# One order of steps for the opening of a hybrid transformer block: products of ones, half of u's first block between v's tiles, two low parts on GpSimd

## The chip, the cores and the metric

The kernel runs on one NeuronCore of a Trainium2 chip. Five engines work side by side, each through its own queue in program order: TensorE (PE, with its weight loads PEld), VectorE (DVE), ScalarE (ACT), GpSimd (POOL) and SyncE (SP, which here issues most DMAs). They meet only through semaphores. The metric is the device time of one execution in microseconds (us), lower is better. The kernel before takes 1760.06 us, the median of three runs (1760.02 to 1760.11).

## The reference

The reference is one layer of a hybrid decoder on x of 1024 rows by 1024 channels, in float32:

```python
h = rms_norm(x, attn_norm_w)
q, k, v, u, g = split(h @ w_in)          # 1024, 1024, 1024, 2048, 2048 columns
a = diff_attention(rms(q), rms(k), v)    # 8 heads, causal, with a position bias
y_a = (rms_norm(a) * (1 - lam_init)) @ w_proj_attn
u_a, u_b = split(u)
c = silu(layer_norm(causal_conv31(u_a * sigmoid(u_b)) + conv_b))
y_b = c @ w_proj_conv
g_a, g_b = split(sigmoid(g + gate_b))
x = x + (g_a * y_a + g_b * y_b) @ w_out
x = x + swiglu(rms_norm(x, ffn_norm_w))  # w_gate_up, w_down
```

The change lies in the first two lines: the row norm, and the first of the products with w_in.

## The kernel before, in words

**Precision.** Every large product is made of three: each operand is split into a high part (a cast to fp32r on ACT, `split_hi`, L119) and a low part (the rest, a subtraction on DVE, `split_lo`, L124), and PE adds high by high, high by low and low by high into one PSUM bank (L152 to L154).

**The opening.** x comes in eight tiles of 128 rows. For each, `xtile` (L622) runs `norm_T` (L606): a square with a row sum on ACT (L609), the row statistic on DVE with a root on ACT (L603, L573 to L578), a multiplication by it and by the norm weights on DVE in two halves (L613), eight transposes on PE (L616), and the split into `hT_hi` and `hT_lo`, the normed rows with channels on the partitions. The norm weights arrive as one load that repeats them on all partitions (`anw_b`, 512 KB, L173, ACT's queue).

**The items.** The first phase walks a list of items: "V0" is 256 columns of v for all eight row tiles (24 products of 256 columns each, `v_item`, L633), "U0" is channels 0 to 127 of u_a and u_b for two blocks of 512 rows (four times 24 products of 512 columns, `u_item`, L539), "Q0" a head of q and k. The list begins V0, U0, U1, V1. V0 prepares the row tiles as it goes. An item stops (yields) after each group of products, and after each stop 3.25 taps of the 31-tap convolution go to DVE. Weights come through `Stream` (L293): a load of 512 KB into one of two raw buffers (`wraw`), then the split; `ahead` says how many are prepared before they are used.

**What sets the order.** The program is recorded, and a scheduler then puts the instructions of each engine in an order, so work of later items can stand between that of earlier ones; `after(ins)` (L126) holds what is recorded inside it behind a given instruction. In the opening before, nothing is held: V's tiles, the preparation of later tiles, U0's products, the small vectors (L200 to L230) and the position bias rows (`bias_rows`, L661) are woven together by the scheduler.

After the first phase come attention with the remaining items (318 to about 825 us), the projections, and the channel mixer.

## Time and profile before

| | us |
|---|---|
| median of three runs | 1760.06 |
| the profiled execution, as a run | 1761.41 |
| its span, first to last instruction | 1759.6 |
| PE busy in the span | 1740.3 |
| DVE busy | 1273.2 |
| ACT busy | 800.5 |
| POOL busy | 26.7 |

Busy time is the sum of an engine's instructions without their overlap. PE's products overlap, so one product's price is read from the distance between two starts. A row of the timeline gives start, duration, engine, source line, operation, output and inputs, shapes, and in square brackets how long the engine had been idle before it and what released it. "xN" merges N like instructions. In lists of waits the columns are total, times, and the longest. A table of windows gives each engine's busy time (and count) per stretch of the span.

### The profile page before, as it was taken

What the parts mean: (1) busy time and instruction counts of PE and PEld (TensorE: products, weight loads), DVE (VectorE), ACT (ScalarE), POOL (GpSimd) and SP (SyncE); (2) the same over time, 40 slices, a digit from 0 to 9 for tenths busy, and PEclk for the clock granted to TensorE, in tenths of its full rate; (3) what the DMA queues carried; (4) which work ended last, traced back from release to release, by engine and by line L of the source; (5) the groups of instructions that cost most, each with busy time, mean ns of one, the idle gap of its engine ahead of it and who ended that gap; (6) DMA issues with size and microseconds to landing.
All of it is one profiled execution on the core that took longest, in us unless ns stands there. A gap on an engine that the chain in (4) does not pass through costs nothing.

```text
span 1759.6 us, 25844 instructions
## 1 busy us (share of the span) xinstructions
PE 1740.3 (99%) x9367; PEld 1503.1 (85%) x9367; DVE 1273.2 (72%) x2187; ACT 800.5 (45%) x1886; POOL 26.7 (2%) x106
## 2 busy tenths in 40 slices
PE   7999999999999999999999999999999999999999
PEld 6898998988999998988888888888888888888887
DVE  6388879999988888886687534877667666664544
ACT  4211241558767776655557313643333333333332
POOL 3000000000000000000000000000000000000000
PEclk9999999999999999999999999999999999999999
DMA  8433353235444344352983544234544544697663
GB/s 248 164 121 114 108 158 124 76 96 151 111 138 124 88 114 138 86 163 76 336 268 108 168 167 144 91 102 146 177 150 158 176 157 139 210 360 242 215 216 131
DMA packets 255728, 275.34 MB, mean 156 GB/s; under 512 B 16064, under 2 KB 177896, under 8 KB 255600
## 3 DMA queue, kind: packets, MB, share of 16 engines
q1 hardware_dynamic: 253568, 267.45, 47.6%
q0 software_dynamic: 1744, 5.19, 1.0%
q8 instruction: 74, 1.21, 0.3%
q10 hardware_dynamic: 288, 1.05, 0.2%
q14 instruction: 54, 0.44, 0.1%
HBM read 176.59 MB, written 78.68 MB: 145 GB/s over the span
## 4 chain that ended last, share of the span: by engine, by line
PE 95%; DMA 2%; ACT 1%; DVE 1%; issue 0%; SPq 0%; ACTq 0%
PE acc L1375 22%; PE pg L153 15%; PE pg L154 15%; PE pg L152 15%; PE acc L451 12%; PE sc L817 2%; PE sc L816 2%; PE wo L154 2%; PE wo L153 2%; PE wo L152 2%; PE pT L852 2%; PE pW L152 1%; PE pW L154 1%; PE pW L153 1%; PE pQ L714 1%; DMA wraw<-in_w_in_dram 1%
## 5 line engine op out<-in xcount | busy, mean ns | idle before, releaser
L525 DVE SCALAR_TENSOR_TENSOR acc<-u,cw,acc 128x1024 f32<-128x1024 f32 x240 | 306.8, 1278 | 2.8
L152 PE MATMUL pg<-whi,hT_hi 128*128 128x256 f32 x768 | 220.3, 287 | 1.2 <-ACT hT_hi L119 1.2
L154 PE MATMUL pg<-whi,hT_lo 128*128 128x256 f32 x768 | 219.8, 286 | 0.4 <-DVE hT_lo L124 0.4
L153 PE MATMUL pg<-wlo,hT_hi 128*128 128x256 f32 x768 | 219.1, 285 | 0.2 <-DVE wlo L124 0.2
L119 ACT CAST whi<-wraw 128x1024 fp32r<-128x1024 f32 x109 | 114.4, 1051 | 215.9 <-PE pg L153 122.1
L152 PE MATMUL pg<-hT_hi,whi 128*128 128x512 f32 x512 | 201.6, 394 | 0.0
L154 PE MATMUL pg<-hT_hi,wlo 128*128 128x512 f32 x512 | 200.9, 393 | 0.0
L153 PE MATMUL pg<-hT_lo,whi 128*128 128x512 f32 x512 | 200.5, 392 | 0.0
L124 DVE TENSOR_TENSOR wlo<-wraw,whi 128x1024 fp32r<-128x1024 f32 x109 | 132.8, 1219 | 70.8 <-ACT whi L119 66.7
L124 DVE TENSOR_TENSOR wlo<-draw,whi 128x1024 fp32r<-128x1024 f32 x75 | 91.8, 1224 | 89.6 <-ACT whi L119 84.3
L152 PEld LDWEIGHTS pg<-whi,hT_hi 128*128 128x128 f32 x768 | 147.7, 192 | 4.2 <-ACT hT_hi L119 2.5
L154 PEld LDWEIGHTS pg<-whi,hT_lo 128*128 128x128 f32 x768 | 147.8, 192 | 2.3 <-DVE hT_lo L124 1.1
L153 PEld LDWEIGHTS pg<-wlo,hT_hi 128*128 128x128 f32 x768 | 147.7, 192 | 2.0 <-DVE wlo L124 0.5
L119 ACT CAST whi<-draw 128x1024 fp32r<-128x1024 f32 x75 | 79.1, 1055 | 129.5 <-PE acc L451 125.9
L451 PE MATMUL acc<-wlo,whi 128*128 128x512 f32 x308 | 119.8, 389 | 0.0
L451 PE MATMUL acc<-whi,wlo 128*128 128x512 f32 x308 | 119.8, 389 | 0.0
L823 ACT ACTIVATE E<-E,mn 128x256 f32<-128x256 f32 (+7 forms) x128 | 99.7, 779 | 35.8 <-DVE mn L818 33.6
L154 PEld LDWEIGHTS pg<-hT_hi,wlo 128*128 128x128 f32 x512 | 96.2, 188 | 19.0
L153 PEld LDWEIGHTS pg<-hT_lo,whi 128*128 128x128 f32 x512 | 96.2, 188 | 18.7
L152 PEld LDWEIGHTS pg<-hT_hi,whi 128*128 128x128 f32 x512 | 96.3, 188 | 18.3
L1375 PE MATMUL acc<-h_hi,whi 128*128 128x512 f32 x240 | 93.4, 389 | 0.0
L1375 PE MATMUL acc<-h_lo,whi 128*128 128x512 f32 x240 | 93.4, 389 | 0.0
(270 smaller groups left out, 3951.5 us busy)
## 6 DMA issues: line engine op xcount, KB each, us to landing
wraw<-in_w_gate_up_dram SPq DMA_DIRECT2D x44, 512.0 KB, 4.8
wraw<-in_w_in_dram SPq DMA_DIRECT2D x40, 512.0 KB, 4.5
qs<-qs SPq DMA_DIRECT2D x96, 128.0 KB, 2.3
wd<-in_w_down_dram SPq DMA_DIRECT2D x44, 256.0 KB, 3.1
tdT<-wd SPq DMA_DIRECT2D x88, 128.0 KB, 4.3
draw<-sdS SPq DMA_DIRECT2D x44, 256.0 KB, 3.8
draw<-tdT SPq DMA_DIRECT2D x44, 256.0 KB, 3.9
wraw<-in_w_in_dram SPq DMA_DIRECT2D x32, 256.0 KB, 3.3
```

The source lines that it names most:

```text
L119: act.copy(dst, src)
L124: last_lo[0] = dve.tensor_tensor(dst, src, f32(hi), op=ALU.subtract).ins
L152: pe.matmul(o, lh, rh, start=start, stop=False)
L153: pe.matmul(o, lh, rl, start=False, stop=False)
L154: last_mm[0] = pe.matmul(o, ll, rh, start=False, stop=stop).ins
L451: m = pe.matmul(o[s_][i][:], l_[:, ts], r_[:, 512:], start=start and j + y_ == 0, stop=j == n - 1 and y_ == 2, skip_group_check=not start,)
L525: dve.scalar_tensor_tensor(acc[0][:], us[c][:, t : t + S], cw[:, c, t : t + 1], acc[0][:], op0=ALU.mult, op1=ALU.add)
L816: pe.matmul(o[:, :w], qh[:, qs], k, start=True, stop=False)
L817: last_mm[0] = pe.matmul(o[:, :w], ql[:, qs], k, start=False, stop=True).ins
L823: act.activation(e[:, :nk], e[:, :nk], AF.Exp, bias=mn[:, j : j + 1], scale=-1.0, accum_out=l[:, j : j + 1])
L852: pe.transpose(pt[:, k * P : (k + 1) * P], e[:, (k0 + k) * P : (k0 + k + 1) * P], ident[:])
L1375: pe.matmul(o[:], a_[x_][:, k, :], b_[y_][:, k, :], start=start and k + x_ + y_ == 0, stop=k == 3 and x_ == 1, skip_group_check=not start,)
```

## The change

It replaces the scheduler's order of V0 and U0 by one that is written out, `opening()`, and takes both from the list. Each of its steps is recorded inside `in_order()`, which holds it behind the last instruction of DVE, ACT and PE recorded so far. Within this:

- the norm weights arrive as two rows of 512 numbers (4 KB together), and PE spreads them over the partitions by a product with a column of ones (`spread_weights`), from where ACT copies them;
- PE multiplies a tile of ones with itself 3, 6 and 8 times (`keep_busy`), into PSUM tiles that nobody reads;
- x's first tile comes in two halves, and its square is shared by ACT and DVE; tiles 2 and 3 share one row statistic, and so do tiles 4 to 7;
- V0's weights get their own tiles, and their two low parts are made by POOL; V's 24 products of a tile are ordered high by high, low by high, high by low over all eight channel groups;
- U0 stands between V's tiles: rows 0 to 511 after V tile 3, rows 512 to 1023 after V tile 7;
- the small vectors' loads move behind POOL's low parts (`load_vectors`), their use behind V's tiles (`vectors`), and the bias rows behind what DVE and POOL had at the 16th stop. The opening stops seven times; V0 and U0 stopped eight times.

The places that the prediction speaks of, as the built programs have them. PE's first rows, before (px are the transposed rows of x's tile 0, pg V's sums):

```order
L616 MATMUL px_7_353<-ident_78,xt0_90 128x128 x4
L616 MATMUL px_8_361<-ident_78,xt0_90 128x128 x4
L152 MATMUL pg_21_398<-whi_10_370,hT_hi_334 128x256
L153 MATMUL pg_21_398<-wlo_11_371,hT_hi_334 128x256
L154 MATMUL pg_21_398<-whi_10_370,hT_lo_335 128x256
L152 MATMUL pg_21_398<-whi_10_370,hT_hi_334 128x256
```

and after, from the second row on; ahead of it stand three products of ones (pm are sums that spread the weights, or of ones):

```order
L200 MATMUL pm_14_347<-anw0_90,one_92 128x512
L200 MATMUL pm_15_350<-anw1_91,one_92 128x512
L196 MATMUL pm_16_355<-busy_93 128x512 x6
L677 MATMUL px_17_366<-ident_78,xt0_98 128x128 x4
L677 MATMUL px_18_372<-ident_78,xt0_98 128x128 x4
L833 MATMUL pg_19_380<-vwh_3_323,hT_hi_308 128x256 x4
L833 MATMUL pg_19_380<-vwh_5_325,hT_hi_308 128x256 x4
L833 MATMUL pg_19_380<-vwh_3_323,hT_lo_309 128x256 x4
L833 MATMUL pg_19_380<-vwh_5_325,hT_lo_309 128x256 x4
L833 MATMUL pg_19_380<-vwl_4_324,hT_hi_308 128x256 x4
L833 MATMUL pg_19_380<-vwl_6_326,hT_hi_308 128x256 x4
L196 MATMUL pm_20_405<-busy_93 128x512 x8
```

The transposes and V's products stand behind nine products of ones; eight more stand between tile 0 and tile 1, and the low parts of the weights (vwl) are used last.

ACT, from the casts of x's tile 3 (px_36, px_37) to u's first sigmoid, after:

```order
L120 CAST hT_hi_308<-px_36_500 128x4x128
L120 CAST hT_hi_308<-px_37_506 128x4x128
L120 CAST whi_39_537<-wraw_38_535 128x1024
L120 CAST whi_42_543<-wraw_41_541 128x1024
L120 CAST vh_45_574<-pg_19_380 128x512
L120 CAST whi_48_582<-wraw_47_580 128x1024
L652 ACTIVATE xj_51_611,ssx_50_610<-xt4_527 128x1024
L652 ACTIVATE xj_52_613,ssx_50_610<-xt5_529 128x1024
L652 ACTIVATE xj_53_615,ssx_50_610<-xt6_531 128x1024
L652 ACTIVATE xj_54_617,ssx_50_610<-xt7_533 128x1024
L609 ACTIVATE t_57_622<-v_55_619 128x4
L120 CAST vh_58_631<-pg_44_547 128x512
```

Before, from the cast of x's tile 4's first half on:

```order
L119 CAST hT_hi_334<-px_50_618 128x4x128
L609 ACTIVATE xj7_770,ss_67_771<-xt7_571 128x1024
L119 CAST vh_43_597<-pg_30_486 128x512
L119 CAST hT_hi_334<-px_51_626 128x4x128
L573 ACTIVATE t_70_776<-v_68_773 128x1
L119 CAST hT_hi_334<-px_56_671 128x4x128
L119 CAST hT_hi_334<-px_57_679 128x4x128
L545 ACT_TABLE_LOAD
L545 ACTIVATE sg_82_866<-pg_81_841 128x512
L119 CAST hT_hi_334<-px_65_731 128x4x128
```

After, the casts of three U weights (whi_39, whi_42, whi_48) stand ahead of the squares of tiles 4 to 7, and one statistic (t_57) serves all four; before, each tile's square and root stood by itself among the casts, and the U weights' casts stood elsewhere. SP's rows at the same place, after; wraw_47 is the load that whi_48 is cast from, and it takes the raw buffer of wraw_38:

```order
L287 DMA wraw_38_535<-in_w_in_dram 128x8x128
L177 DMA xt4_527<-in_x_dram 128x1024
L287 DMA wraw_41_541<-in_w_in_dram 128x8x128
L177 DMA xt5_529<-in_x_dram 128x1024
L177 DMA xt6_531<-in_x_dram 128x1024
L177 DMA xt7_533<-in_x_dram 128x1024
L287 DMA wraw_47_580<-in_w_in_dram 128x8x128
L694 DMA v_hi0_110<-vh_45_574 128x2x256
```

DVE, from the end of the row statistic of tiles 4 to 7 to the norm of tile 7, after:

```order
L614 TENSOR_TENSOR r_56_621<-r_56_621,t_57_622 128x4
L667 SCALAR_TENSOR_TENSOR xt4_527<-xt4_527,r_56_621,anw_b_101 128x512 x2
L125 TENSOR_TENSOR vl_59_632<-pg_44_547,vh_58_631 128x512
L667 SCALAR_TENSOR_TENSOR xt5_529<-xt5_529,r_56_621,anw_b_101 128x512 x2
L125 TENSOR_TENSOR hT_lo_309<-px_62_666,hT_hi_308 128x4x128
L125 TENSOR_TENSOR hT_lo_309<-px_63_672,hT_hi_308 128x4x128
L579 TENSOR_TENSOR sg_61_662<-pg_66_692,sg_61_662 128x512
L125 TENSOR_TENSOR hT_lo_309<-px_64_680,hT_hi_308 128x4x128
L125 TENSOR_TENSOR hT_lo_309<-px_65_686,hT_hi_308 128x4x128
L667 SCALAR_TENSOR_TENSOR xt6_531<-xt6_531,r_56_621,anw_b_101 128x512 x2
L667 SCALAR_TENSOR_TENSOR xt7_533<-xt7_533,r_56_621,anw_b_101 128x512 x2
```

Before, from the norm of tile 7 to u's first product with the sigmoid:

```order
L613 SCALAR_TENSOR_TENSOR xt7_571<-xt7_571,r_69_775,anw_b_92 128x512 x2
L124 TENSOR_TENSOR hT_lo_335<-px_56_671,hT_hi_334 128x4x128
L124 TENSOR_TENSOR hT_lo_335<-px_57_679,hT_hi_334 128x4x128
L124 TENSOR_TENSOR hT_lo_335<-px_65_731,hT_hi_334 128x4x128
L124 TENSOR_TENSOR vl_59_711<-pg_45_603,vh_58_710 128x512
L124 TENSOR_TENSOR hT_lo_335<-px_66_739,hT_hi_334 128x4x128
L124 TENSOR_TENSOR hT_lo_335<-px_71_784,hT_hi_334 128x4x128
L124 TENSOR_TENSOR hT_lo_335<-px_72_792,hT_hi_334 128x4x128
L124 TENSOR_TENSOR wlo_20_389<-wraw_18_386,whi_19_388 128x1024
L124 TENSOR_TENSOR vl_74_824<-pg_60_716,vh_73_823 128x512
L124 TENSOR_TENSOR wlo_77_832<-wraw_75_829,whi_76_831 128x1024
L548 TENSOR_TENSOR sg_82_866<-pg_83_868,sg_82_866 128x512
```

After, u's product with the sigmoid (sg_61, of u's sum pg_66) stands ahead of tile 5's low parts and of the norms of tiles 6 and 7; before, all norms and low parts stood ahead of it. On PE, after, the transposes of tiles 4 and 5 stand between u's first two groups of 24 products, and those of tiles 6 and 7 behind the second.

The diff, cut to its core:

```diff
+    @contextmanager
+    def in_order():
+        E = mybir.EngineType
+        with after(last_of(E.DVE)), after(last_of(E.Activation)), after(last_of(E.PE)):
+            yield
...
-    xload(0)
+    anw = [ap.tile([P, 512], F32R, tag="vh", name=f"anw{g}")[0:1, :].bitcast(F32) for g in range(2)]
+    one = ap.tile([1, P], F32, name="one", bufs=1)
+    busy = ap.tile([P, 512], F32R, tag="vl", name="busy")
+    dve.memset(f32(busy[:]), 1.0)
+    dve.memset(one[:], 1.0)
+    for g in range(2):
+        nc.scalar.dma_start(anw[g], attn_norm_w[:, 512 * g : 512 * (g + 1)])
+    xts[0] = ap.tile([P, D], F32, tag="xt", name="xt0", bufs=4)
+    for g in range(2):
+        nc.sync.dma_start(xts[0][:, 512 * g : 512 * (g + 1)], xs[0:P, 512 * g : 512 * (g + 1)])
     wb = ap.tile([P, D], F32, name="anw_b", bufs=1)
-    nc.scalar.dma_start(wb[:], attn_norm_w.to_broadcast([P, D]))
+    def keep_busy(n):
+        pt = pm()
+        for _ in range(n):
+            pe.matmul(pt[:], busy[:, :P], busy[:], start=True, stop=True)
+    def spread_weights(g):
+        pt = pm()
+        pe.matmul(pt[:], one[:], anw[g], start=True, stop=True)
+        act.copy(wb[:, 512 * g : 512 * (g + 1)], pt[:])
...
+    def load_vectors():
+        pool.memset(rows[:], 0.0)
+        pool.dma_start(cwrow[:], conv_w[0])
+        vec_rows("conv_b", conv_b, 8)
...
-    first = ["V0", "U0", "U1", "V1", "U2", "U3", "V2", "U4", "Q0", "V3", "U5", "U6", "U7"]
+    first = ["U1", "V1", "U2", "U3", "V2", "U4", "Q0", "V3", "U5", "U6", "U7"]
...
+    def u_half(c, w, sb):
+        cs = slice(sb * 512, (sb + 1) * 512)
+        ob = gemm_T(w[0], hT_hi, hT_lo, sb)
+        sg = wp.tile([P, 512], F32, tag="sg", name=nm("sg"), bufs=2)
+        act.activation(sg[:], ob[:], AF.Sigmoid)
+        yield
+        oa = gemm_T(w[1], hT_hi, hT_lo, sb)
+        dve.tensor_tensor(sg[:], oa[:], sg[:], op=ALU.mult)
+        nc.sync.dma_start(u_d[c][:, cs], sg[:])
+        if sb == 1:
+            bg.todo.insert(max(0, len(bg.todo) - CW), conv_load(c))
+            bg.add(conv_taps(c))
+        yield
     def u_item(c):
-        wb_, wa_ = ws.next(), ws.next()
+        w = ws.next(), ws.next()
         for sb in range(2):
...
+            yield from u_half(c, w, sb)
...
+    rx = {}
+    def stats(tiles):
+        n = len(tiles)
+        ss = sm.tile([P, 4], F32, tag="ssx", name=nm("ssx"), bufs=2)[:, :n]
+        for j, i in enumerate(tiles):
+            junk = ap.tile([P, D], F32, tag="junk", name=nm("xj"), bufs=1)
+            src = xts[i]
+            if i:
+                act.activation(junk[:], src[:], AF.Square, accum_out=ss[:, j : j + 1])
+            else:
+                s2 = sm.tile([P, 1], F32, tag="ss", name=nm("ss"), bufs=1)
+                act.activation(junk[:, :512], src[:, :512], AF.Square, accum_out=ss[:, j : j + 1])
+                dve.tensor_tensor_reduce(
+                    junk[:, 512:], src[:, 512:], src[:, 512:], 1.0, 0.0, ALU.mult, ALU.add, accum_out=s2[:]
+                )
+                dve.tensor_tensor(ss, ss, s2[:], op=ALU.add)
+        r = rstd_of(ss, n, 1.0 / D)
+        for j, i in enumerate(tiles):
+            rx[i] = r[:, j : j + 1]
+    def norm(i):
         for g in range(2):
-            half, gs = hbuf(g), slice(512 * g, 512 * (g + 1))
-            dve.scalar_tensor_tensor(half, src[:, gs], r, wb[:, gs], op0=ALU.mult, op1=ALU.mult)
-            pt = tp()
+            half, gs = xts[i][:, 512 * g : 512 * (g + 1)], slice(512 * g, 512 * (g + 1))
+            dve.scalar_tensor_tensor(half, half, rx[i], wb[:, gs], op0=ALU.mult, op1=ALU.mult)
+    def turn_x(i):
+        for g in range(2):
+            pt = pxp.tile([P, 512], F32, tag="px", name=nm("px"))
             for k in range(4):
-                pe.transpose(pt[:, k * P : (k + 1) * P], half[:, k * P : (k + 1) * P], ident[:])
+                c0 = 512 * g + k * P
+                pe.transpose(pt[:, k * P : (k + 1) * P], xts[i][:, c0 : c0 + P], ident[:])
             src4 = pt[:].rearrange("p (k s) -> p k s", s=P)
-            h_ = hi[:, 4 * g : 4 * g + 4, i * P : (i + 1) * P]
+            h_ = hT_hi[:, 4 * g : 4 * g + 4, i * P : (i + 1) * P]
             split_hi(h_, src4)
-            split_lo(lo[:, 4 * g : 4 * g + 4, i * P : (i + 1) * P], src4, h_)
+            turned[i, g] = src4, h_
+    def low_x(i):
+        for g in range(2):
+            src4, h_ = turned.pop((i, g))
+            split_lo(hT_lo[:, 4 * g : 4 * g + 4, i * P : (i + 1) * P], src4, h_)
...
+    def opening():
+        nonlocal qkp
+        raws = [wraw(), wraw()]
+        for g, raw in enumerate(raws):
+            nc.sync.dma_start(
+                raw[:].rearrange("p (k c) -> p k c", c=256),
+                win[512 * g : 512 * (g + 1), V0 : V0 + 256].rearrange("(k p) c -> p k c", p=P),
+            )
+        for i in range(1, 4):
+            xload(i)
+        wv = [[vw.tile([P, 1024], F32R, tag=t_, name=nm(t_)) for t_ in ("vwh", "vwl")] for g in range(2)]
+        halves = [[t_[:].rearrange("p (k c) -> p k c", c=256) for t_ in w] for w in wv]
+        uw, o = [], {}
+        def wv_hi(g):
+            split_hi(wv[g][0][:], raws[g][:])
+            pool.tensor_tensor(wv[g][1][:], raws[g][:], f32(wv[g][0][:]), op=ALU.subtract)
+        def v_tile(i):
+            if i % 2 == 0:
+                o[i // 2] = pg()
+            ts, dst = slice(i * P, (i + 1) * P), o[i // 2][:, 256 * (i % 2) : 256 * (i % 2 + 1)]
+            terms = [(k, a_, b_) for a_, b_ in ((0, 0), (1, 0), (0, 1)) for k in range(NKT)]
+            for n_, (k, a_, b_) in enumerate(terms):
+                l_, r_ = (hT_hi, hT_lo)[a_][:, k, ts], halves[k // 4][b_][:, k % 4, :]
+                last_mm[0] = pe.matmul(dst, l_, r_, start=n_ == 0, stop=n_ == len(terms) - 1).ins
+        def steps(*fns):
+            for fn in fns:
+                with in_order():
+                    fn()
+        def weight():
+            uw.append(ws.next())
+        steps(
+            lambda: keep_busy(3),
+            lambda: stats([0]),
+            lambda: spread_weights(0),
+            lambda: spread_weights(1),
+            lambda: norm(0),
+            lambda: keep_busy(6),
+            lambda: wv_hi(0),
+            lambda: wv_hi(1),
+            lambda: turn_x(0),
+            lambda: low_x(0),
+            lambda: v_tile(0),
+            lambda: keep_busy(8),
+            lambda: stats([1]),
+            lambda: norm(1),
+            lambda: stats([2, 3]),
+            lambda: turn_x(1),
+            lambda: low_x(1),
+            lambda: v_tile(1),
+            lambda: norm(2),
+            lambda: turn_x(2),
+            lambda: norm(3),
+            lambda: low_x(2),
+            lambda: turn_x(3),
+        )
+        with after(last_of(mybir.EngineType.Pool)):
+            load_vectors()
+        for i in range(4, NT):
+            xload(i)
+        steps(
+            weight,
+            lambda: v_tile(2),
+            lambda: low_x(3),
+            lambda: v_split(o[0], 0, 0),
+            weight,
+        )
+        yield
+        steps(
+            lambda: v_tile(3),
+            lambda: stats([4, 5, 6, 7]),
+            lambda: norm(4),
+            lambda: v_split(o[1], 0, 1),
+        )
+        yield
+        first_half, second_half = u_half(0, uw, 0), u_half(0, uw, 1)
+        steps(lambda: next(first_half), lambda: norm(5), lambda: turn_x(4), lambda: low_x(4), lambda: turn_x(5))
+        yield
+        steps(
+            lambda: next(first_half),
+            lambda: low_x(5),
+            lambda: norm(6),
+            lambda: turn_x(6),
+            lambda: norm(7),
+            lambda: low_x(6),
+            lambda: turn_x(7),
+            lambda: low_x(7),
+            lambda: v_tile(4),
+            lambda: v_tile(5),
+        )
+        yield
+        v_split(o[2], 0, 2)
+        steps(lambda: v_tile(6), lambda: v_tile(7), vectors)
+        v_split(o[3], 0, 3)
+        yield
+        vw_ctx.close()
+        qkp = qk_ctx.enter_context(tc.tile_pool(name="qkp", bufs=2, side="right", reuse_waits="tile"))
+        ws.ahead = 2
+        yield from second_half
+    ws.ahead = 1
     n = 0
     due = 0.0
-    for _ in run(first):
+    for _ in chain(opening(), run(first)):
         n += 1
         if n == 16:
-            bias_rows()
+            with after(last_of(mybir.EngineType.DVE)), after(last_of(mybir.EngineType.Pool)):
+                bias_rows()
         if n >= 18 and n % 3 == 0 and (n - 18) // 3 < H:
             bias_skew((n - 18) // 3)
         due += TAPS_FIRST
```

139 lines of the change are left out of this document (54 added, 85 removed).

## The prediction

> **What bounds the kernel now.** I read the page's head first, then the table of windows, then PE's waits, then the opening in order of time.
>
> ```profile
> span 1759.6 us, 25844 instructions
> core 0: us, PE busy (x) PEld busy (x) DVE busy (x) ACT busy (x) POOL busy (x), PEclk, DMA share, GB/s
> 0.00:10.00 10.00, 0.55 (x3) 0.58 (x4) 2.35 (x8) 2.63 (x4) 6.08 (x17) 1.00 0.83 218
> 10.00:20.00 10.00, 8.80 (x39) 7.64 (x37) 7.57 (x23) 7.99 (x15) 3.44 (x9) 1.00 1.01 338
> 20.00:36.00 16.00, 15.35 (x113) 12.57 (x112) 14.95 (x49) 9.25 (x21) 2.24 (x5) 1.00 0.58 179
> 36.00:94.00 58.00, 58.00 (x317) 50.40 (x315) 23.75 (x32) 15.05 (x24) 2.40 (x5) 1.00 0.55 176
> 260.00:830.00 570.00, 566.48 (x3682) 513.48 (x3681) 499.80 (x1087) 356.06 (x1201) 12.12 (x68) 1.00 0.40 117
> ```
>
> From 36 us on TensorE (PE) is busy all the time: whatever makes its opening work end earlier or later moves the end of the kernel by as much. In the opening it loses time in three ways: it starts late, it starts slowly, and it waits a little.
>
> ```profile
> PE px L616 <- DVE xt L613: 9.4, 1, 9.4
> 12.37 0.58 PE L152 MATMUL pg<-whi,hT_hi 128*128 128x256 f32 x1 [0.98 <-ACT hT_hi L119]
> 17.96 0.41 PE L152 MATMUL pg<-whi,hT_hi 128*128 128x256 f32 x1
> 18.17 0.41 PE L153 MATMUL pg<-wlo,hT_hi 128*128 128x256 f32 x1
> 22.00 0.28 PE L154 MATMUL pg<-whi,hT_lo 128*128 128x256 f32 x1
> 22.12 0.28 PE L152 MATMUL pg<-whi,hT_hi 128*128 128x256 f32 x1
> 39.06 0.39 PE L152 MATMUL pg<-hT_hi,whi 128*128 128x512 f32 x1
> 39.29 0.39 PE L153 MATMUL pg<-hT_lo,whi 128*128 128x512 f32 x1
> 93.78 0.28 PE L152 MATMUL pg<-whi,hT_hi 128*128 128x256 f32 x1
> ```
>
> The first row is from PE's waits (total, times, longest), the others give an instruction's start and duration. Products overlap, so the price of one is the distance between starts: 0.21 us for 256 columns at 18 us, 0.12 us at 22 us, 0.23 us for 512 columns. The first products ran at half rate, though the windows show PEclk 1.00 throughout; that column does not show this slow start. The last row is the first product of V1, the first item behind V0, U0 and U1. **I measure both kernels to this point.** V0 is 192 products (22.9 us at 0.119), U0 and U1 are 192 of 512 columns (43.7 us at 0.228). With 64 transposes, the small vectors and the bias rows that is about 76 us of work, so PE had lost some 18 us by 93.78. That is all a better opening could win; the change wins if it loses less.
>
> **The change part by part.** The 17 products of ones and the two that spread the norm weights cost nothing while PE has no rows to work on. The broadcast load of 512 KB goes, and most of POOL's small loads leave the front.
>
> ```profile
> 6.02 1.06 ACT L609 ACTIVATE xj<-xt 128x1024 f32<-128x1024 f32 x1 [4.00 <-DMA xt<-in_x_dram]
> 7.20 0.15 DVE L603 TENSOR_SCALAR v<-ss 128x1 f32<-128x1 f32 x1 [7.20 <-ACT xj L609]
> 8.60 1.41 DVE L613 SCALAR_TENSOR_TENSOR xt<-xt,r,anw_b 128x512 f32<-128x512 f32 x2
> 10.78 1.04 ACT L119 CAST whi<-wraw 128x1024 fp32r<-128x1024 f32 x1 [3.19 <-DMA wraw<-in_w_in_dram]
> 12.22 1.05 ACT L119 CAST whi<-wraw 128x1024 fp32r<-128x1024 f32 x1
> 13.18 0.58 ACT L119 CAST hT_hi<-px 128x512 fp32r<-128x512 f32 x1
> 2.64 0.31 POOL masks.py:199 TENSOR_SCALAR_AFFINE_SELECT ident<-ident 128x128 f32<-128x128 f32 x1
> ```
>
> Tile 0's products waited for V0's weights (10.78) more than for the row (8.60). About 0.6 MB fewer bytes stand ahead of these weights now; at the 338 GB/s of the window that is nearly 2 us, so I put them at 9.0 and 10.4 (bounds: 7.5 and 8.9, or the old times). A full cast takes ACT 0.96 us (12.22 to 13.18). ACT casts the weights first, to 11.4, then tile 0's two halves, 0.48 each: tile 0's products start at 12.0, hardly before the 12.37 us of now.
>
> **The low parts on POOL** have no row like them. The floor is DVE's own 1.23 us for this subtraction; above it, POOL's select above takes 0.31 us for 128 columns, about 0.1 of it start, so 1.8 us for 1024, and twice the operands make at most 3.5. I take 2.6, nearer the select, and keep 1.2 and 3.5. Two in a row from 10.1 end at 15.3, and tile 0 at 15.9, the last products having waited 0.8 us. (The Trainium skill's GPSIMD Engine Reference, Performance versus the Vector engine, has a two-input add of 2048 columns at 4497 ns against 2293 on DVE; half of that, an estimate, would be 2.25 us and the sum 0.7 us less. No row here shows it.)
>
> **One order of steps** is where the price lies. Rows for its links:
>
> ```profile
> 14.84 1.06 ACT L609 ACTIVATE xj<-xt 128x1024 f32<-128x1024 f32 x1
> 25.53 0.59 ACT L119 CAST vh<-pg 128x512 fp32r<-128x512 f32 x1
> 26.01 0.60 ACT L119 CAST hT_hi<-px 128x512 fp32r<-128x512 f32 x1
> 28.57 0.68 DVE L124 TENSOR_TENSOR vl<-pg,vh 128x512 fp32r<-128x512 f32 x1
> 29.17 0.68 DVE L124 TENSOR_TENSOR hT_lo<-px,hT_hi 128x512 fp32r<-128x512 f32 x1
> 30.34 1.41 DVE L613 SCALAR_TENSOR_TENSOR xt<-xt,r,anw_b 128x512 f32<-128x512 f32 x2
> 43.06 1.04 PE L616 MATMUL px<-ident,xt 128*128 128x128 f32 x8
> 60.39 1.23 DVE L124 TENSOR_TENSOR wlo<-wraw,whi 128x1024 fp32r<-128x1024 f32 x1 [0.26 <-ACT whi L119]
> 65.42 0.69 DVE L548 TENSOR_TENSOR sg<-pg,sg 128x512 f32<-128x512 f32 x1 [3.80 <-PE pg L154]
> wraw<-in_w_in_dram SPq DMA_DIRECT2D x40, 512.0 KB, 4.5
> xt<-in_x_dram SPq DMA_DIRECT2D x8, 512.0 KB, 5.8
> ```
>
> So: a square 1.06, the statistics behind it 1.4 (7.20 to 8.60), a half cast 0.48, a half low part 0.60, a tile's norm 1.3, its eight transposes 0.8, a weight's low part 1.2, a weight's load 4.5 us. The path, in us from the start:
>
> - Eight products of ones (1.8) to 17.7, tile 1's transposes to 18.4, casts to 19.3, low parts to 20.2, norms of tiles 2 and 3 (2.7) to 22.9, the last transposes to 23.3, casts to 24.4.
> - ACT casts U0's first weight to 25.4, DVE makes its low part to 26.6. PE has V tiles 2 and 3 to do meanwhile, and waits 1.4 us in tile 3, whose low parts stand on DVE behind both weights' low parts. Then u's first half block runs from 30.5 to 36.0.
> - **First stall.** SP's next weight load needs the raw buffer that the low part frees: issued at 26.7, landed at 31.2. Behind it on SP stand only stores of V and later weights. ACT's cast of it stands ahead of the squares of tiles 4 to 7, whose rows are there by then (tile 7's load is issued when tile 3 is turned, at 23.6, and takes 5.8 at the median). So the cast ends at 32.2, the squares at 36.4, the statistics at 38.0, norm 4 at 39.3, a low part of V at 39.9, norm 5 at 41.3, its transposes at 41.7. PE, done at 36.0, did nothing but 1.4 us of transposes since: about 4.3 us lost.
> - **Second stall.** PE runs the other 24 products (5.5) to 47.2. DVE's product with the sigmoid (0.3 to be released, 0.6 itself) stands ahead of tile 5's low parts (1.2) and the norms of tiles 6 and 7 (2.7): 52.0, the transposes 52.5. PE had only these 1.4 us in between: about 3.9 us lost.
> - V tiles 4 to 7 (96 products, 11.4) to 63.9, the vectors 0.9 to 64.8, U0's second block (48, 10.9) to 75.7, U1 (21.9) to **97.6**.
>
> ```profile
> 25.24 1.45 PE L672 MATMUL pm<-oh,rb 33*8 33x384 f32 x4
> 26.62 0.39 PE L152 MATMUL pg<-whi,hT_hi 128*128 128x256 f32 x1
> 29.38 0.81 PE L672 MATMUL pm<-oh,rb 33*8 33x384 f32 x2
> 30.12 0.38 PE L154 MATMUL pg<-whi,hT_lo 128*128 128x256 f32 x1
> ```
>
> Before, the bias rows' 1.4 and 0.7 us lie ahead of 93.78; after, they come later in the first phase. They are work either way, so the fair point of before is 93.78 - 2.1 = 91.7. The change is **97.6 - 91.7 = 5.9 us slower**. The profiled execution took 1761.4 us in all, 1.8 outside its span; the runs' median is 1760.06. A difference inside the span adds to either: 1760.06 + 5.9 = **1766.0**.
>
> Costed at nothing: the opening now yields 7 times, not 8, so three conv taps of some 1.3 us move from the first phase, where DVE has slack, into attention, most of the window from 260 to 830, where PE idles only 3.5 of 570 us and DVE 70; that slack hides them, without it they would cost up to 4 us, and the reshuffled order there may give or take 1. The bias rows' DMAs now come later, but their first reader is in attention, over 100 us on.
>
> **The rivals.**
>
> *Not slower.* One mechanism: the raw buffer. If the third U weight's load is not what ACT waits for, because the front runs early and the buffer is free by some 22 us, the squares start right after V's first cast at 26.8, tiles 4 and 5 are turned under u's first half, and the first stall is nearly gone. That takes 4.3 off, and the front 2.5 more (weights 1.5 earlier, POOL at DVE's pace 0.8): 5.9 - 6.8, about **1759**. For it: the load's 4.5 is a median, and the DMA engines are 58% busy from 20 to 36 us. Against it: the order puts two norms, four casts and a weight's low part ahead of the load's issue. For over 0.2% faster the second stall would have to shrink as well, and no row allows that.
>
> *The clock falls back.* PE ran at half rate for 8 us after its first long run of products (12.37 to past 20). If pauses like the two stalls bring that back, each half block behind a stall takes 11 us instead of 5.5, at worst: 4 to 8 us more, about **1772**. The row that speaks for it is the late start of the full rate; the longest pause of PE once warm in this trace is under 1 us, so none speaks directly. (By the Trainium skill, TensorE: Matmul & The Clock Gate, Part 1, the rate falls after a whole idle window of some 3.4 us and rises after a busy one. By that rule neither pause, broken up by transposes, is long enough, and 1766 stands. But the trace's slow spell, about 8 us, is longer than that page's window.)
>
> *The ones do not help.* The six products wait for the first copy of spread weights (a PSUM buffer), and if the full rate comes only at 18 us, tile 0 and the eight products run at 0.21 and 0.43: 2 us more, **1768**.
>
> **How the numbers follow.** The path as worked out: 0.55, with its own range 1762.5 to 1769.3 (weights 1.5 earlier, POOL at 1.2, the load at 3.3: minus 3.5; POOL at 3.5, the load at 5.5, weights 0.5 later: plus 3.3). Not slower: 0.27. Clock falls back: 0.12. Ones do not help: 0.06. The range, 1760.0 to 1771.5, cuts off half of the second case and part of the third. Faster or slower by 0.2% (3.5 us) is what a measurement of this kernel can tell from none: faster 0.10, out of the not-slower case; same 0.22, the rest of it and the path's lower edge; slower 0.68.
>
> **What would show it.** Two PE waits of about 2 to 3 us each, one for DVE's norm of tile 4 after u's first half, one for the norm of tile 6 after the second, would confirm the stalls; ACT's cast of a U weight released by its DMA near 31 us, the first cause. V1's first product near 97.6 confirms the sum. A POOL low part far from 2.6 us, products at 0.21 us after 20 us, or V1's first product ahead of 93 would each make it wrong.

## The result, and the profile after

The change makes the kernel slower: 1786.01 us (median of four runs, 1785.69 to 1789.12) against 1760.09 us, a ratio of 1.0146 with a 95% interval of 1.0134 to 1.0158. The forecast was 1766.0, with a range up to 1771.5. The profiled execution took 1789.12 us, its span is 27.5 us longer than that of before. A repeat of the same kernel (below, after_again) took 1785.51 us, 24.7 over before on its chip.

Where the time went is read from points that both programs have: the first product of V1, the first product of attention's scores (sc), the first product of the projection behind attention (aTh), and the start of the last products. First the kernel before, the views of two tiles (duration least/median/most in ns, first and last start in us), then the kernel after, with the row of V1:

```profile
L816 PE MATMUL sc<-ks,qs x192: 220/389/497, 318.5 to 813.8; 128*128 128x512 f32 x96, 128*128 128x128 f32 x32, 128*128 128x256 f32 x32, 128*128 128x384 f32 x32
L152 PE MATMUL pg<-aTh,whi x128: 387/389/799, 847.4 to 939.0; 128*128 128x512 f32 x128
```

```profile
105.05 0.28 PE L160 MATMUL pg<-whi,hT_hi 128*128 128x256 f32 x1
L974 PE MATMUL sc<-ks,qs x192: 220/389/501, 332.4 to 835.1; 128*128 128x512 f32 x96, 128*128 128x128 f32 x32, 128*128 128x256 f32 x32, 128*128 128x384 f32 x32
L160 PE MATMUL pg<-aTh,whi x128: 387/389/799, 871.9 to 964.9; 128*128 128x512 f32 x128
```

| stretch | before | after | more |
|---|---|---|---|
| start to V1's first product | 93.8 | 105.05 | 11.3 |
| to the first score | 224.7 | 227.3 | 2.6 |
| attention, to the next projection | 528.9 | 539.5 | 10.6 |
| next three parts | 323.0 | 324.4 | 1.4 |
| first T1h product to the last start | 584.5 | 586.4 | 1.9 |

Attention ends here at the first product of the next projection; T1h (and T4h below) are differences of the channel mixer's rows. The 2.6 are mostly the bias rows' 2.1 us, which have moved behind V1. So the opening costs 13.9, and as much again is lost behind 318 us, where the diff moves next to nothing.

The opening after, in order of time (start, duration, engine, line, operation, [idle before, and what released it]):

```profile
30.85 0.40 PE L160 MATMUL pg<-hT_hi,whi 128*128 128x512 f32 x1
33.03 1.05 ACT L120 CAST whi<-wraw 128x1024 fp32r<-128x1024 f32 x1 [5.92 <-DMA wraw<-in_w_in_dram]
38.70 0.17 DVE L639 TENSOR_SCALAR v<-ssx 128x4 f32<-128x4 f32 x1 [3.37 <-ACT xj L652]
41.00 1.94 PE L677 MATMUL px<-ident,xt 128*128 128x128 f32 x8 [4.52 <-issue]
44.14 1.97 PE L677 MATMUL px<-ident,xt 128*128 128x128 f32 x8 [1.20 <-DVE hT_lo L125]
52.16 0.69 DVE L579 TENSOR_TENSOR sg<-pg,sg 128x512 f32<-128x512 f32 x1 [7.48 <-PE pg L162]
54.81 1.33 PE L677 MATMUL px<-ident,xt 128*128 128x128 f32 x8 [2.69 <-issue]
57.35 1.96 PE L677 MATMUL px<-ident,xt 128*128 128x128 f32 x8 [1.21 <-DVE hT_lo L125]
58.95 2.02 PE L833 MATMUL pg<-vwh,hT_hi 128*128 128x256 f32 x8
72.28 0.50 PE L160 MATMUL pg<-hT_hi,whi 128*128 128x512 f32 x1
```

Both stalls of the prediction are there, made as it said: the third U weight's cast, released by its DMA, ahead of four squares; the sigmoid product ahead of the norms. Two things are more than forecast. Each tile's transposes wait for the low parts of the tile before (1.20 and 1.21 us), which still hold the two PSUM buffers. And three of the four sets of eight transposes take some 1.95 us instead of 1.1: PE runs at half rate. The windows of the same stretch show it (PE busy, its clock, DMA share, GB/s):

```profile
40.00:44.00 4.00, 1.94 (x8) 0.54 0.39 133
44.00:48.00 4.00, 3.86 (x15) 0.60 0.00 0
56.00:60.00 4.00, 2.79 (x15) 0.68 0.01 4
60.00:64.00 4.00, 4.00 (x32) 0.90 0.00 0
```

In attention PE waits longer than in the kernel before, where each pause was 0.8 us at most; some of the waits of after (total, times, longest), and what the clock does behind them (the waits of 1.2 and 0.6 us lie between 651 and 656 us, those of 1.6 at 839 and 870):

```profile
PE pT L1010 <- DVE E L990: 1.6, 1, 1.6
PE sc L974 <- DMA ks<-klo: 1.2, 1, 1.2
PE sc L975 <- DMA qs<-qs: 0.6, 1, 0.6
PE pg L160 <- ACT aTh L120: 1.6, 1, 1.6
656.00:660.00 4.00, 4.00 (x26) 0.73 0.00 0
844.00:848.00 4.00, 4.00 (x25) 0.76 0.01 4
872.00:876.00 4.00, 4.00 (x11) 0.65 1.05 398
```

But the slow spells are the smaller part, and they don't follow every such wait. Two waits and a window of no_stalls (below), which has the same order in attention, and behind them a window of warm:

```profile
PE pT L1010 <- DVE E L990: 1.6, 1, 1.6
PE pg L160 <- ACT aTh L120: 1.5, 1, 1.5
828.00:832.00 4.00, 3.38 (x27) 1.00 0.01 4
832.00:836.00 4.00, 3.38 (x20) 0.73 0.48 155
```

In no_stalls the clock stayed at 1.00 throughout attention, behind both waits (they end at 826.8 and 856.5), and attention still took 535.7 us: PE stood still for 8.4 us of it, against 3.5 of 528.9 before. In after it stood still for 9.8, and busy time times what the clock lacked adds 3.0 (windows from 652 to 660 and from 840 to 848).

### The profile page after: what moved, and what is told of

Same layout as the page of the kernel before. It is cut to its first block, busy times and chain, and to the rows that moved or that the text cites. A ratio compares the mean times of both kernels' runs of the same rounds, so it can differ in the third digit from the quotient of the medians.

```text
span 1787.1 us, 25860 instructions
## 1 busy us (share of the span) xinstructions
PE 1759.1 (98%) x9388; PEld 1512.3 (85%) x9388; DVE 1270.7 (71%) x2166; ACT 801.1 (45%) x1884; POOL 31.2 (2%) x108
## 3 DMA queue, kind: packets, MB, share of 16 engines
q8 instruction: 74, 1.21, 0.3%
## 4 chain that ended last, share of the span: by engine, by line
PE 90%; DMA 3%; DVE 3%; ACT 2%; issue 1%; SPq 1%; POOL 0%; ACTq 0%
PE acc L1533 21%; PE pg L160 14%; PE pg L161 14%; PE pg L162 14%; PE acc L484 12%; PE wo L160 2%; PE wo L161 2%; PE wo L162 2%; PE sc L975 2%; PE sc L974 1%; DMA vl<-v_lo 1%; PE pT L1010 1%; DMA qs<-qs 1%; PE pg L833 1%; PE pW L162 1%
## 5 line engine op out<-in xcount | busy, mean ns | idle before, releaser
L162 PE MATMUL pg<-whi,hT_lo 128*128 128x256 f32 x704 | 201.0, 286 | 0.0
L161 PE MATMUL pg<-wlo,hT_hi 128*128 128x256 f32 x704 | 200.8, 285 | 0.0
L160 PE MATMUL pg<-whi,hT_hi 128*128 128x256 f32 x704 | 200.2, 285 | 0.4 <-ACT jk L748 0.4
L160 PEld LDWEIGHTS pg<-whi,hT_hi 128*128 128x128 f32 x704 | 134.9, 192 | 2.6 <-ACT jk L748 0.8
L162 PEld LDWEIGHTS pg<-whi,hT_lo 128*128 128x128 f32 x704 | 135.1, 192 | 0.9
L161 PEld LDWEIGHTS pg<-wlo,hT_hi 128*128 128x128 f32 x704 | 135.0, 192 | 0.9
```

The source lines that it names most:

```text
L160: pe.matmul(o, lh, rh, start=start, stop=False)
L161: pe.matmul(o, lh, rl, start=False, stop=False)
L162: last_mm[0] = pe.matmul(o, ll, rh, start=False, stop=stop).ins
```

## The experiments

Four causes were taken apart: the opening's order of steps, attention's order of instructions, the addresses of tiles, and the single parts of the change. Times are medians, "over before" is against the kernel before on the same chip.

| run | time | over before | ratio, 95% | V1 at | attention | last part |
|---|---|---|---|---|---|---|
| after_again | 1785.51 | 24.7 | 1.0125-1.0152 | 105.07 | 537.2 | 587.0 |
| same_order | 1782.90 | 20.6 | 1.0097-1.0128 | 111.7 | 529.1 | 586.3 |
| aligned | 1780.52 | 19.8 | 1.0094-1.0122 | 105.5 | 535.5 | 584.9 |
| warm | 1778.26 | 16.0 | 1.0070-1.0104 | 102.1 | 533.4 | 588.0 |
| order_only | 1777.38 | 16.7 | 1.0087-1.0117 | 104.23 | 529.2 | 586.4 |
| order_pad | 1774.58 | 13.9 | 1.0066-1.0099 | 104.84 | 528.1 | 584.6 |
| no_stalls | 1774.12 | 11.8 | 1.0052-1.0084 | 93.47 | 535.7 | 586.8 |
| woven_dve_low | 1765.70 | 5.0 | 1.0013-1.0031 | 96.36 | 527.4 | 585.6 |
| before_ones | 1762.39 | 1.6 | 0.9998-1.0017 | 94.27 | 528.0 | 584.6 |
| before_fewer | 1762.32 | 0.0 | 0.9991-1.0010 | 93.93 | 529.7 | 584.6 |
| tuned | 1761.09 | 0.3 | 0.9994-1.0012 | 88.82 | 528.4 | 586.2 |
| woven_held | 1760.84 | 0.1 | 0.9989-1.0006 | 90.31 | 528.1 | 584.5 |
| woven_no_ones | 1760.71 | 0.0 | 0.9988-1.0007 | 90.23 | 529.3 | 584.6 |
| dve_low_held | 1760.46 | -0.4 | 0.9989-1.0007 | 90.36 | 527.7 | 584.8 |

### The opening: the two stalls

**no_stalls.** Squares and one norm go ahead of the weight's cast, the norms ahead of the sigmoid product.

```diff
             lambda: v_split(o[0], 0, 0),
+            lambda: stats([4, 5, 6, 7]),
+            lambda: norm(4),
             weight,
...
-            lambda: next(first_half),
             lambda: low_x(5),
             lambda: norm(6),
+            lambda: norm(7),
+            lambda: next(first_half),
             lambda: turn_x(6),
-            lambda: norm(7),
             lambda: low_x(6),
```

> The changed kernel with the squares of tiles 4 to 7 and the norm of tile 4 ahead of the cast of the third U weight on ACT and its low part on DVE, and low part 5 and norms 6 and 7 ahead of DVE's sigmoid product. Attention's order stays exactly that of the changed kernel. Theory A (the two PE pauses of 4.5 and 2.7 us are made by these two places in the order of steps, and the half rate behind them by the pauses): PE waits only about 1 us between the transposes of tiles 4 and 5, and of 6 and 7, the transposes take 1.1 us each again instead of 1.95, the first product of V1 comes near 94.5 instead of 105.05, the time is near 1775.5. Theory B (the third weight's late landing at 33.0 is what matters, or squares wait as long for tiles 6 and 7 as they did for the cast): the first pause stays above 3 us and V1 stays above 100.

```profile
36.60 1.03 PE L677 MATMUL px<-ident,xt 128*128 128x128 f32 x8
38.65 1.25 PE L677 MATMUL px<-ident,xt 128*128 128x128 f32 x8 [1.02 <-DVE hT_lo L125]
47.23 1.25 PE L677 MATMUL px<-ident,xt 128*128 128x128 f32 x8 [0.96 <-DVE hT_lo L125]
93.47 0.28 PE L160 MATMUL pg<-whi,hT_hi 128*128 128x256 f32 x1
```

Theory A holds: two lines that change places are worth 11.6 us at V1's first product. Behind pauses of 1.0 us the transposes stay at full rate. The weight whose cast held all this up is U1's first, which PE doesn't read in the changed kernel before some 83 us (72.28, and 10.9 for U0's second block).

**warm.** The stalls stay, PE multiplies ones meanwhile.

```diff
             lambda: norm(5),
+            lambda: keep_busy(19),
             lambda: turn_x(4),
             lambda: low_x(4),
+            lambda: keep_busy(7),
             lambda: turn_x(5),
...
+            lambda: keep_busy(12),
             lambda: turn_x(6),
             lambda: norm(7),
             lambda: low_x(6),
+            lambda: keep_busy(6),
```

> The changed kernel with products of ones on PE inside the two pauses (19 and 7 around tile 4's and 5's transposes, 12 and 6 around tile 6's and 7's). The waits themselves stay. As a side effect attention gets the order of the run before_fewer. Theory A (after a pause PE runs at half rate for some us): the transposes take 1.1 us instead of 1.95, the first products of u's second half and of V's tile 4 run at .23 and .12 us, and the first product of V1 comes 3.5 to 4.5 us earlier than 105.05. Theory B (those rows are slow for another reason, say PSUM or the weights' loads): V1's first product stays within 1 us of 105. If attention's time goes by its order alone, the stretch from the first scores to the next projection equals that of before_fewer within 1 us.

```profile
40.74 1.34 PE L677 MATMUL px<-ident,xt 128*128 128x128 f32 x8
43.88 1.25 PE L677 MATMUL px<-ident,xt 128*128 128x128 f32 x8 [0.18 <-DVE hT_lo L125]
```

The half rate is gone, V1's first product comes 2.95 us earlier, a little less than expected. So the pauses make the slow spells, and in that execution they cost some 3 of the 7.5 us by which the opening missed its forecast. Attention took 533.4 us where before_fewer, in the same order, takes 529.7: order alone doesn't set it. In warm the tiles lie 32 bytes off (below), the wait for aTh is 1.7 us instead of 0.4, and the clock falls to 0.73 at 832 us, behind waits of 1.0 and 0.6.

**after_again.** The changed kernel once more.

> The changed kernel, nothing altered, to have its own profile beside those of the runs around it, since its first profiled execution was 3 us over its others. If the 539.5 us of attention in that first profile are its order and its addresses, they come again within 1 us; if 4 of them were that execution's pauses on a lowered clock (no_stalls 535.7 and aligned 535.5 have the same order), attention takes about 536 here and the price of the order is 7 and not 10.6 us. The last part stays at 586.4 (addresses).

```profile
31.25 1.05 ACT L120 CAST whi<-wraw 128x1024 fp32r<-128x1024 f32 x1 [3.94 <-DMA wraw<-in_w_in_dram]
39.22 1.34 PE L677 MATMUL px<-ident,xt 128*128 128x128 f32 x8 [2.54 <-issue]
44.00:48.00 4.00, 4.00 (x12) 0.50 0.00 0
56.00:60.00 4.00, 3.25 (x16) 0.50 0.02 4
```

Here the weight landed 1.8 us earlier, and the first pause was 2.54 instead of 4.52 us; V1's first product came at 105.07 all the same, because PE was on half clock for longer. Attention, 537.2, lies between the two expectations: with the same order it took 535.5 to 539.5 in four profiled executions (after, after_again, no_stalls, aligned). The next three parts took 322.7 here, so the 1.4 us that the first profile has there belong to its slow spell at 872.

### Attention: its order

The change never touches attention. But the scheduler that orders it starts from what the opening leaves: the count of stops (seven instead of eight, so that one conv tap more is left over, 110 instead of 109), the running count of small PSUM tiles (five more, and attention takes these tiles in turn from three places), and the bias rows' place. In the traces 1680 of PE's 7542 instructions and 476 of DVE's 1893 from the first score on stand out of the sequence of before. Three lines give the old order back, row for row:

```diff
-    n = 0
-    due = 0.0
+    n = 1
+    due = TAPS_FIRST
...
-            with after(last_of(mybir.EngineType.DVE)), after(last_of(mybir.EngineType.Pool)):
-                bias_rows()
+            bias_rows()
...
     a0.close()
+    npm[0] += 1
```

**same_order** is the changed kernel with these.

> The changed kernel, with three things in it that touch no work of the opening but give the attention part exactly the order of instructions that it has before the change: the counter of stops starts at one with 3.25 taps owed, the bias rows are not held behind DVE's and POOL's last instruction, and the running count of small PSUM tiles is moved by one ahead of attention. Measure: from the first product of scores to the first product of the next projection, 528.9 us before (318.5 to 847.4) and 539.5 after (332.4 to 871.9). Theory A (the 10.6 us lost there come from the order that these three side effects of the change give to attention's instructions): that stretch is 529 +-1.5 again, the first product of V1 stays at 105 to 107 (2 of it the bias products, which may come earlier again), and the time is near 1775. Theory B (attention is slower because it starts late, on a lower clock that the two stalls of the opening leave behind): the stretch stays near 539 and the time at 1785 to 1788.

Attention took 529.1: theory A for that stretch. But the time is 1782.9 and not 1775, since the opening was hurt, which was not expected: V1 at 111.7. Freed of its hold, DVE's scaling of the bias table slipped into tile 0's statistics, beside POOL's low parts; first POOL's row, then DVE's:

```profile
9.14 4.64 POOL L824 TENSOR_TENSOR vwl<-wraw,vwh 128x1024 fp32r<-128x1024 f32 x2 [5.83 <-ACT vwh L120]
9.16 2.35 DVE L715 TENSOR_SCALAR rb<-rb 33x8 f32<-33x8 f32 x1 [2.67 <-DMA rb<-in_rel_bias_dram]
11.61 2.20 DVE L612 SCALAR_TENSOR_TENSOR t<-v,t 128x1 f32<-128x1 f32 x1
```

**order_only** mends that: the bias rows are held behind the opening's last DVE instruction.

```diff
+        opened.append(last_of(mybir.EngineType.DVE))
         yield from second_half
...
+            with after(opened[0]):
                 bias_rows()
```

> The changed kernel with attention's order of before and nothing else: as in same_order, but with the bias rows held behind the opening's last DVE instruction, so that the opening isn't hurt. Tiles stay 32 bytes off. If order, addresses and opening are three separate prices: V1's first product at 105.1, attention 530 +-1.5 instead of 537.2 to 539.5, the last part still 586.4 to 587, the time near 1777.5 (8 less than the changed kernel's 1785.5). If attention's loss came from the addresses, attention stays above 535.

```profile
L978 PE MATMUL sc<-ks,qs x192: 220/389/500, 331.5 to 827.1; 128*128 128x512 f32 x96, 128*128 128x128 f32 x32, 128*128 128x256 f32 x32, 128*128 128x384 f32 x32
L160 PE MATMUL pg<-aTh,whi x128: 387/389/799, 860.7 to 952.1; 128*128 128x512 f32 x128
PE sc L978 <- DVE mn L980: 0.8, 1, 0.8
```

529.2 us, and 8 us off the time (1785.5 to 1777.4): the order is worth that much. No wait in attention is longer than 0.8 us now, and the clock stays at 1.00 there.

**before_fewer** is the other side: the kernel before, with one stop less counted.

```diff
-    n = 0
-    due = 0.0
+    n = -1
+    due = -TAPS_FIRST
```

> The kernel before with one thing: the counter of stops and the taps owed start one stop lower, so that one conv tap more is left for attention and the bias rows come one stop later. Nothing of the opening changes. Attention's instructions then stand in another order than in either kernel (about 28% of PE's rows and 29% of DVE's are placed elsewhere). Theory A (order): the first product of V1 comes at 93.8 less up to 2.1 for the bias, the stretch from the first scores to the next projection is not 528.9 but off by several us, up or down, and the time with it. Theory B (late opening and clock): the stretch stays at 529 +-1 and the time within 1 us of 1760; one tap of about 1 us on DVE changes nothing.

529.7 and no difference in time: theory B's numbers, although 2175 of PE's 7542 instructions stood out of the old sequence. Another order need not cost anything; the change's was a poor draw.

### The tiles' addresses

The change makes the pool of small tiles 32 bytes smaller. Behind it nearly all tiles moved off multiples of 64 bytes. A row of before and two of after_again, products whose weights (the 128x128 operand) are sh and sl, the high and low part of a block of the channel mixer's weights:

```profile
L1375 PE MATMUL acc<-T4h,sh x80: 389/389/389, 1188.3 to 1549.8; 128*128 128x512 f32 x80
```

```profile
L1533 PE MATMUL acc<-T4h,sh x80: 393/396/502, 1210.3 to 1574.1; 128*128 128x512 f32 x80
L1533 PE MATMUL acc<-T4h,sl x80: 389/394/398, 1210.7 to 1574.6; 128*128 128x512 f32 x80
```

**aligned** changes one number in the changed kernel, **order_pad** the same in order_only.

```diff
-    sm.tile([P, 32], F32, name="pad_sm", bufs=1)
+    sm.tile([P, 40], F32, name="pad_sm", bufs=1)
```

> The changed kernel with one thing: the padding tile of the small-tile pool is 40 words instead of 32. The change has made that pool 32 bytes smaller, so that nearly every tile behind it (sh and sl, E, ph, pl, vh, vl, tb, wd and others) starts 32 bytes off a multiple of 64; with the pad they start on multiples of 64 again, as in the kernel before. No instruction and no order changes. Theory A (the 128x512 products that read sh and sl take .393 to .396 us instead of .389 because of the address): .389 again, the last part (first T1h product to the end) takes 584.5 us instead of 586.4, and the time falls by about 2 us to 1784; attention, whose tiles move as well, may give back up to 1 more. Theory B (the .007 us are a matter of the clock or of neighbours): nothing changes, 586.4 and 1786.

> order_only with the pad of 40 words as well, so that the opening's order of steps is all that is left of the change's loss. If the prices are separate: V1's first product at 105.1, attention 528.5 +-1, the last part 584.6, the end near 1768.5 and the time near 1774.5; what is left to 1760.8 is then the opening alone, 11.3 us at V1's first product and 2.6 behind it for the bias products. Rival: an execution that was pushed off full rate by the opening's pauses keeps some of it, and the time stays above 1777.

```profile
L1533 PE MATMUL acc<-T4h,sh x80: 389/389/497, 1208.8 to 1570.6; 128*128 128x512 f32 x80
```

The fence is of aligned: 0.389 us again. The last part takes 584.9 and 584.6 us, the time falls by 2.8 us (order_only to order_pad) and by 5.0 (after_again to aligned). The last part's 1.9 and 2.1 us of either are mostly the 240 products that read sh and sl: by the distance between starts they hold 1.5 and 1.4. Attention gives 1.1 and 1.8; which tiles give the rest was not taken apart. order_pad came out at 1774.58, as expected from three separate prices.

### All together, and the parts of the change

**woven_held** has the steps of no_stalls, the pad, attention's order, and the later tiles turned one at a time:

```diff
-            lambda: turn_x(4), lambda: low_x(4), lambda: turn_x(5))
+            lambda: turn_x(4), lambda: low_x(4))
...
+            lambda: turn_x(5),
+            lambda: low_x(5),
+            lambda: v_tile(4),
             lambda: turn_x(6),
             lambda: low_x(6),
+            lambda: v_tile(5),
...
+            lambda: turn_x(7),
+            lambda: low_x(7),
```

> All causes taken away together: the changed opening with squares and norms as in no_stalls and, besides, the transposes of tiles 4 to 7 one tile at a time between u's halves and V's tiles, so that the casts and low parts of one tile lie beside products; the bias rows held behind the opening's last DVE instruction; the counter and the count of small PSUM tiles as in same_order, so that attention has exactly the order of the kernel before; the pad of aligned. If the four parts add up: V1's first product 93.5 less two waits of 1.0 = 91.4; 227.3 from there to the scores; 529 for attention; 92.1 + 87.1 + 143.7 + 584.5 behind it; the end at 1755.1 against 1754.9 before, that is a time within 1.5 us of the kernel before. If they don't add up (attention is slower because of where the opening leaves the queues, as warm's 533.4 against before_fewer's 529.7 in the same order may say): 3 to 5 us more.

```profile
90.31 0.28 PE L160 MATMUL pg<-whi,hT_hi 128*128 128x256 f32 x1
L983 PE MATMUL sc<-ks,qs x192: 220/389/496, 317.7 to 811.8; 128*128 128x512 f32 x96, 128*128 128x128 f32 x32, 128*128 128x256 f32 x32, 128*128 128x384 f32 x32
L160 PE MATMUL pg<-aTh,whi x128: 387/389/799, 845.8 to 937.2; 128*128 128x512 f32 x128
```

With these causes taken away the loss is gone: the time is that of the kernel before. With order and addresses mended it was 1774.6 (order_pad), so the other 13.8 us were the opening's steps, of which woven_held has more than the two stalls changed: its later tiles are turned one at a time, without the 1 us waits of no_stalls.

**woven_no_ones** leaves out the 17 products of ones (`keep_busy(3)`, `(6)`, `(8)`).

> The kernel woven_held without the 17 products of ones (the four that spread the norm's weights stay). The price of the ones alone. Theory A (they bring the full rate forward): tile 0's transposes and its 24 products run at the half rate, .21 instead of .13 us, some 2 to 3 us more of which the wait for tile 1's norm (products from 17.9) hides about 1.5: V1's first product 0.5 to 2 us later than in woven_held. Theory B (PE waits for the rows whatever its rate): V1's first product within 0.3 us.

```profile
11.39 2.08 PE L835 MATMUL pg<-vwh,hT_hi 128*128 128x256 f32 x8 [1.20 <-ACT hT_hi L120]
15.82 1.33 PE L677 MATMUL px<-ident,xt 128*128 128x128 f32 x8
```

Theory B: V1's first product at 90.23 against 90.31. Tile 0's products do run slowly, but tile 1's transposes begin at 15.8 instead of 16.5, where eight ones stood in their way. **before_ones** puts 15 ones into the kernel before:

```diff
     xload(0)
+    keep_busy(15)
```

> The kernel before with 15 products of ones ahead of tile 0's transposes (1.5 to 9.5 us) and the count of small PSUM tiles moved by two, so that attention keeps its order. Theory A (in the opening the rows decide and not PE's rate): tile 0's products run at .13 instead of .21 us and end near 15.8 instead of 18.6, but tile 1's norm ends at 18.65 in the kernel before and holds its transposes; only those gain (.4): V1's first product at 93.3 to 93.8 against 93.78, the time within 0.7 us of before. Theory B (the slow spell from 12.4 to 20.1 is lost time): V1's first product 2.5 to 4 us earlier and the time with it.

```profile
1.45 5.21 PE L177 MATMUL pm<-busy 128*128 128x512 f32 x15 [1.45 <-DVE busy L172]
9.56 1.27 PE L625 MATMUL px<-ident,xt 128*128 128x128 f32 x8 [2.90 <-issue]
16.11 0.41 PE L152 MATMUL pg<-whi,hT_hi 128*128 128x256 f32 x1
16.33 0.41 PE L153 MATMUL pg<-wlo,hT_hi 128*128 128x256 f32 x1
```

V1 at 94.27, half a us later, nothing gained. But this run decides nothing: the ones ended at 6.7 us, not at 9.5, PE stood still for 2.9 us ahead of the transposes and again behind them, and tile 0's products ran at 0.21 us until 18.2 all the same. The rate that the ones were to bring was not there. That the rows decide and not PE's rate is shown by woven_no_ones for the changed opening, and not shown for the kernel before.

**woven_dve_low** makes V's two low parts on DVE.

```diff
-            pool.tensor_tensor(wv[g][1][:], raws[g][:], f32(wv[g][0][:]), op=ALU.subtract)
+            split_lo(wv[g][1][:], raws[g][:], wv[g][0][:])
```

> The kernel woven_held with the two low parts of V's first weights on DVE (1.23 us each by the profile) instead of POOL (2.37 each). Theory A (POOL's work is not beside DVE's for nothing: while it runs, DVE instructions with two operands from SBUF stand still, .85 us for a 128x1 product in the changed kernel's trace): no DVE instruction of 128x1 takes over .3 us there, the wait for the weights' low part (.36) is gone, DVE's low parts of tile 0 come .7 us later; V1's first product within 0.7 us of woven_held, so the move to POOL was worth nothing. Theory B (POOL takes 2.5 us of work off the engine that decides): V1's first product 1.5 to 2.5 us later.

```profile
14.55 1.04 ACT L120 CAST vwh<-wraw 128x1024 fp32r<-128x1024 f32 x1 [3.92 <-DMA wraw<-in_w_in_dram]
```

Neither theory: 6 us later, since the second weight landed at 14.5 instead of 9.15. The vectors' loads stand behind POOL's last instruction; without low parts on POOL they go out from 2.5 us on. **dve_low_held** gives POOL something to wait for:

```diff
+        with after(last_of(mybir.EngineType.Pool)):
+            pool.tensor_copy(turn[:], f32(wv[1][1][:, :8]))
```

> The kernel woven_dve_low, with POOL made to wait: it copies 128x8 of the weights' low part before it issues the loads of the vectors, so that they come behind the first weights as in woven_held. In woven_dve_low POOL had nothing to wait for, issued them from 2.5 us on, and V's second weight block landed 12.4 us after its issue instead of 7.0; V1's first product came at 96.36. Theory A (those loads were the 6 us): the casts of V's weights start near 7.8 and 9.15 again, the first product of V1 comes within 0.7 us of woven_held's 90.31, and low parts on POOL are worth nothing by themselves. Theory B (low parts on DVE cost the time): V1 stays above 94.

90.36: theory A. What the move to POOL brought was its delay of the small loads, not its arithmetic.

**tuned** weaves tiles 2 and 3 too.

```diff
             lambda: low_x(2),
+            lambda: v_tile(2),
             lambda: turn_x(3),
+            lambda: low_x(3),
...
-            lambda: stats([4, 5, 6, 7]),
+            lambda: stats([4, 5]),
```

> The kernel woven_held with tiles 2 and 3 one at a time as well (transposes, low part, products, then the next tile), five ones instead of eight ahead of tile 1, the third U weight's cast behind all squares, and the squares of tiles 4 and 5 apart from those of 6 and 7. The waits of .97 and .80 us go, and tile 2's products start at 20.9 instead of 23.7: u's first half near 27.7 instead of 30.7, V1's first product near 87.3 instead of 90.31, the end at 1750 against 1754.9 before: some 3 us less than woven_held, ratio to before 0.998. Rival: tile 7 of x lands near 29.5 or the weights' casts come in the way, so that u's halves wait 2 to 3 us and the time is woven_held's.

V1's first product gained 1.5 us, half of what was expected, and the time nothing: in the profiled execution PE waits 1.3 us for DVE near 1528 us. No version tried beats the kernel before by what can be measured.

## Why the prediction was wrong

**Right:** the direction, the measuring point for the opening, and both stalls with their causes. u's first half began at 30.85 (forecast 30.5), the low parts on POOL took 2.37 us (2.6), V's weights were cast at 8.26 and 9.57 (9.0 and 10.4), and the wait in V tile 3 was 0.80 (1.4). The front, then, was well sized.

Of the 20 us that the forecast lacked, the opening holds 7.5, attention's order 8 and the addresses 2.8 to 5.

**Wrong, the stalls' size.** V1's first product came at 105.05, not 97.6: 7.5 us, already whole at u's second half block (72.28 against 64.8). The step that failed first is the rate behind the stalls. The path priced everything behind a pause at full rate; "the clock falls back" stood only among the rivals, priced at 4 to 8 us and given 0.12, and it was right, beside the stalls. From the windows of after, the busy time times what the clock lacked is 0.9 + 1.5 + 0.9 + 0.4 = 3.7 us; the same working gives 5.5 for the repeat; warm took 2.95 off. By the Trainium skill's rule (TensorE: Matmul & The Clock Gate, Part 1) the prediction held both pauses for too short. Of the pauses that came, only the one of 4.5 us is longer than that rule's window; for the others the trace disagrees, with clocks of 0.68 behind 2.7 and 1.2 us, of 0.50 to 0.64 behind 2.5 and 1.8 in the repeat, and of 0.58 behind 1.57 and 0.61 in attention (aligned).

The pauses themselves came near their forecast: 9.6 us in the first profile and 7.8 in the repeat, against 8.2. They were made in part by something that the path left out, the two PSUM buffers of the transposes (waits of 1.20 and 1.21 us), where the path let tile 5's transposes follow norm 5. The load (4.5 forecast) took 6.1 us in the first profile and 4.1 in the repeat. Pauses and clock together are 13.3 and 13.2 us, which is why V1 came at the same time in both. Without them there are 60.8 us from u's first product to V1's in both profiles, where the path has 58.9: some 1.9 us of work were priced too low, and which was not taken apart. So the 7.5 us of the first profile are, to 0.2 us, 3.7 for the clock, 1.4 for the pauses, 1.9 for work, and 0.35 for the later start of u.

**Wrong, "costed at nothing".** The prediction said that PE's busy time carries the opening's loss unchanged to the end, and that the reshuffled order in attention "may give or take 1". It took 8 us (order_only). One tap was moved, not three, and neither it nor DVE's slack was the matter (before_fewer moves the same tap at no price): the scheduler drew another order for over a fifth of PE's instructions, with pauses of 1.2 to 1.7 us, and slow spells behind some of them.

**Missed altogether:** the addresses, 2.8 to 5 us. Nothing in the profile of before speaks of them; the diff does, in the small tiles of the row sums and in the pads that stand in the kernel.

**The other rivals.** "Not slower" by the raw buffer: the load was what ACT waited for. "The ones do not help": true in the changed opening, at a price of nothing instead of 2 us (woven_no_ones).

## What to carry to other kernels

A prefetch on an engine's queue may not stand ahead of work that the next product needs: here the cast of a weight that is read 50 us later, and a product that nobody waits for ahead of two norms, cost 11.6 us. After any edit ahead of a scheduled part, compare that part's order and the tiles' addresses with the old ones before reading its time as the edit's. Then mend one cause per run: here 24.7 us fell apart into 13.8 for the opening, 7.9 for the order and 2.8 for the addresses.
